# Second output block with six products by seven, second down block with sixteen; weight sums of three pairs by adding transfers

## The chip, the cores and the metric

The kernel runs on one core of one Trainium2 chip. The metric is the device time of one execution in microseconds, the median of several runs. A profiled execution gives the trace: its span goes from the first to the last instruction, and its own time is a little longer than the span.

## The reference

One layer of a hybrid block for 256 tokens of width 2048, all in fp32:

```python
h = rms_norm(x, g_mix);  proj = h @ w_in          # 2048 x (queries, keys, values, gates)
o_fox, o_sb, o_mem = three attentions over slices of proj
merged = g0 * (o_fox @ w_br_fox) + g1 * (o_sb @ w_br_sb) + g2 * (o_mem @ w_br_mem)
x = x + merged @ w_out                            # 2048 x 2048
h2 = rms_norm(x, g_ffn)
u = causal_depthwise_conv(h2 @ w_up, conv_w, conv_b)   # 2048 x 11264
u_gate, u_val = split(u)
return x + (silu(u_gate) * u_val) @ w_down        # 5632 x 2048
```

## The kernel before

All weights stream from memory in pieces of 128 rows by 1024 columns (0.5 MB in fp32). TensorE multiplies fp32 as two parts: ScalarE (ACT) makes the high part of a piece by a cast (`hi`), VectorE (DVE) the low part by a subtraction (`lo`), and each product of a 128x128 block of activations with a half piece of 512 columns is `three` matmuls: high by high, low activation by high weight, high activation by low weight. There are four buffers each for `hi` and `lo`, and six for the raw pieces.

The stages by the trace: projections, attentions and gates until about 659 us; the output stage `o` (merged @ w_out) in two blocks of 1024 columns, 659 to 700 and 700 to 742 us; the up stage `u` with its convolution, 742 to 1232 us, 176 pieces; the down stage `d` in two blocks, 1232 to 1344 and 1344 to 1455 us.

`blocked()` does a block of the stages `o` and `d`. It takes the weights' row tiles in pairs, 8 pairs in `o` and 22 in `d`, and a string, the plan, says for each pair in which way it is multiplied:

- `e`, `eight`: the 2x2 blocks of 128 tokens and 512 columns for two row tiles, 8 products, 24 matmuls; two pieces are loaded.
- `s`, `seven`: the same by seven products (after Strassen and Winograd), 21 matmuls of 128x512. It needs sums of weights T1 to T4 and sums of activations FS1 to FS4, and loads three and a half pieces: `raw0` (half a piece of weights and T3), `raw1`, `raw_t` (T1 and T2) and T4. Products go to four more PSUM banks Y, which `gather` adds to the output behind the last seven of a block.
- `f`, `form`: no product; it makes the sums of activations of the next pair (`pair_sums`: five steps on DVE with further splitting steps, and casts on ACT). In the output stage the sums of activations are made by `merged_sums` and `last_merged_sums`.

The weight sums do not depend on the activations. They are made beforehand, as background work, and kept in memory (`kept_...`): a pair's two pieces are loaded into SBUF (`pre_...`), DVE adds three times, and the four sums are stored. `halves` lists the pairs, output stage first; `first_sums`, `pair_sums_ahead` and `half_sums` work the list off, the last part of it during the up stage, one pair every 8 ticks (a tick there is one weight piece). All those transfers are issued by SyncE (SP) in one queue, the one that carries the weight pieces too.

In `o`'s second block the residual x of the first block is complete, and `hidden_T` transposes it (hT, 16 transposes on TensorE into four banks, read by ACT and DVE, L183 and L186, while ACT also squares x for the norm, L622); the four banks are then used for Y. Most instructions may be reordered by a scheduler; those in `in_order` stay where they are.

Of the kernel before, what the change touches and what calls it, by code (L numbers as in the profile page):

```python
# [10 lines left out]
F32 = mybir.dt.float32  # L11
F32R = mybir.dt.float32r
AF = mybir.ActivationFunctionType
ALU = mybir.AluOpType
AX = mybir.AxisListType

P = 128
# [16 lines left out]
PIECE = 1024  # L34
# [9 lines left out]
def hybrid_block(  # L44
# [25 lines left out]
    nc = tc.nc  # L70
# [31 lines left out]
    background = []  # L102
# [72 lines left out]
    def split_to(dst, src):  # L175

        nc.scalar.copy(dst[..., :S], src)
        nc.vector.tensor_tensor(dst[..., S:], src, dst[..., :S].bitcast(F32), ALU.subtract)
# [25 lines left out]
    def k_tiles(name):  # L204
# [19 lines left out]

    o_plans = ("eessssse", "eessssse")
    g_plans = (("", "esesesee", "esesesee"), ("esesesee", "esesesee", "esesesee"))
    d_plans = (
        "efefefef" + "sef" * 4 + "ssefsfssfssee",  # L230
        "efefef" + "sss" + "esss" * 3 + "ssee",
    )
    T1, T3, T4, T2 = range(4)
    FS2, FS4, FS3, FS1 = range(4)
    in_order = tc.keep_in_program_order
    dram = ctx.enter_context(tc.tile_pool(name="dram", bufs=1, space=bass.MemoryType.DRAM))
    by_k = lambda w: w[0].rearrange("(k p) n -> p k n", p=P)
    o_sevens = (0, 1, 2, 3, 6)
    pairs = lambda name, n: o_sevens if name == "o" else range(n)
    sums_of = {}  # L240
    ordered = [False]
    halves = deque(
# [1 line left out]
        for name, w, plans in (("o", w_out, o_plans), ("d", w_down, d_plans))  # L244
        for nb, plan in enumerate(plans)
        for pr in pairs(name, plan.count("s"))
        for h in range(2)
    )

# [35 lines left out]
    def pair_sums_ahead(staging, period, add, store, most=99, delay=0):  # L285

        due = deque()
        clock = 0
        for _ in range(delay):
            yield  # L290

        def step():
            while due and due[0][0] <= clock:
                _, kept, w = due.popleft()
                in_order(nc.sync.dma_start(kept, w))

        periods = cycle(period if isinstance(period, tuple) else (period,))
        while len(halves) > 1 and halves[0][-1] == 0 and most:
            most -= 1
            name, wv, nb, pr, _ = halves.popleft()  # L300
            halves.popleft()
            kept = kept_for(name, nb, pr)
            w = staging(f"pre_{name}{nb}_{pr}")
            in_order(
                nc.sync.dma_start(
                    w.rearrange("p (k c) -> p k c", k=2), wv[:, 2 * pr : 2 * pr + 2, nb * PIECE : (nb + 1) * PIECE]
                )
            )
            w = w.rearrange("p (i c) -> p i c", i=4)
            due.append((clock + store, kept, w))  # L310
            for t in range(next(periods)):
                if t == add:
                    sums_in(w)
                step()
                clock += 1
                yield
        while due:
            step()
            clock += 1
            yield  # L320

    def first_sums():

# [319 lines left out]
    def block(name, dt=F32):  # L643
        return bp.tile([P, 1024], dt, tag="blk", name=name)
# [409 lines left out]
    def last_merged_sums():  # L1054
        yield 2
        after = op.tile([P, KT, 2 * S], F32R, tag="ot", name="m_after")
        ms[6] = after[:, 0:2].rearrange("p k c -> p (k c)").rearrange("p (f l q) -> p f l q", f=4, l=2)
        pair_sums(mT[6], block("mw_6"), [(ms[6], slice(0, 4))])

    raw_g = lambda name: wp.tile([P, PIECE], F32, tag="raw", name=name)  # L1060

# [117 lines left out]
    for nb, plan in enumerate(o_plans):  # L1179
# [20 lines left out]
    background.append(  # L1200
        pair_sums_ahead(lambda name: ends_tile(name, F32).rearrange("p i c -> p (i c)"), 8, 1, 5, delay=DU)
    )

    def a_pair(p):
        if p < FA // 2:
            return aT[:, 2 * p : 2 * p + 2]
        if not ends:
            ends.append(ends_tile("a_ends", F32R).rearrange("p i (k c) -> p i k c", k=2))
        return ends[0][:, p - FA // 2]
# [22 lines left out]
    def taken(cr, y, f, s):  # L1232
        ct = s * FT + f
        u = pads[f % 2]
        ins = nc.vector.tensor_tensor(u[:, 2:], cr, rbc, ALU.mult)  # L1235
        if y is not None:
            in_order(ins)
        y = y_tile(f, s) if y is None else y
        tap = lambda j: taps[:, j, ct : ct + 1]
        nc.scalar.activation(y, u[:, 2:], AF.Identity, scale=tap(2), bias=tap(3))  # L1240
        nc.vector.scalar_tensor_tensor(y, u[:, 1 : S + 1], tap(1), y, ALU.mult, ALU.add)
        nc.vector.scalar_tensor_tensor(y, u[:, 0:S], tap(0), y, ALU.mult, ALU.add)
        if s == 0:
            nc.scalar.activation(y, y, AF.Silu)
            ys[f] = y
        else:
            g = ys.pop(f)
            nc.vector.tensor_tensor(g, g, y, ALU.mult)
            split_to(a_pair(f // 2)[:, f % 2], g)

    def conv(ps, f, s):
        taken(out_of(ps, cp.tile([P, S], F32, tag="cr", bufs=2, name=f"cr_{f}_{s}")), None, f, s)
# [66 lines left out]
    def s_of(p, f):  # L1319


        if f == FS1:
            return a_blocks[:, 2 * p, :, 1]
        if p < 9:
            return sf[:, 3 * p + f]
        if p == 9:
            return sf_more[0][:, f] if f < 2 else sf_rest[2]
        if p == 10:
            return sf[:, 27] if f == 0 else sf_rest[f - 1]
        return a_blocks[:, 2 * (p - N0 + N1) + f // 2, :, f % 2]  # L1330

    tmp_d = lambda name: place([P, PIECE], F32, "ts", name)

# [66 lines left out]
```

## Time and profile before

| | us |
|---|---|
| median of 3 runs | 1460.83 (1460.07 to 1462.5) |
| profiled execution, own time | 1460.56 |
| its span | 1458.8 |
| TensorE busy | 1452.1 |
| VectorE busy | 1221.8 |
| ScalarE busy | 851.9 |
| GpSimd busy | 21.4 |

The granted TensorE clock was 1.000. In the lines of the profile, `hi_o`, `lo_o`, `raw_o` are the pieces of the output stage, `_u` of the up stage, `_d` of the down stage, and `hi_t`, `lo_t`, `raw_t` the sums of weights. A group's line gives its count, busy time, mean duration of one, and the idle time of the engine ahead of it with what ended most of it. A line of the timeline gives start, duration and, in brackets, the engine's idle time before it and its releaser; the matmuls' ends are modelled and overlap the next starts.

### The profile page before, as it was taken

To read this page: it belongs to the slowest core of one execution; us is meant where nothing else is said; L and a number is where in the kernel's file an instruction comes from. 1 tells how busy PE (TensorE), PEld (TensorE's weight loads), DVE (VectorE), ACT (ScalarE), POOL (GpSimd) and SP (SyncE) were. 2 spreads that over 40 slices of the span, in tenths; PEclk is the share of its full clock that TensorE was granted. 3 is DMA by queue.
4 is the path that set the end of the run, shared out by engine and by line. 5 is a ranking of instruction groups with operands and counts; after the bars stand their busy time and mean duration, and the time that the engine had idled before them with its cause. 6 is when DMAs were issued, how large, how long until landed. Compare 5 with 4: busy or idle time off the path is not lost.

```text
span 1458.8 us, 20569 instructions
## 1 busy us (share of the span) xinstructions
PE 1452.1 (100%) x7295; PEld 1228.4 (84%) x7295; DVE 1221.8 (84%) x1804; ACT 851.9 (58%) x1210; POOL 21.4 (1%) x52
## 2 busy tenths in 40 slices
PE   9999999999999999999999999999999999999998
PEld 7888878888888888888888888888888888888887
DVE  5788778776898899998987888888888877999878
ACT  6755445464564555546766656556556565676665
POOL 0000010010000000000000000000000000000000
PEclk9999999999999999999999999999999999999999
DMA  8797899777668576788877888888888866789896
GB/s 290 228 352 247 320 323 333 266 250 217 212 206 268 176 226 201 271 266 261 304 213 231 290 275 299 282 270 299 286 278 298 272 197 201 253 283 341 293 334 220
DMA packets 166502, 387.64 MB, mean 266 GB/s; under 512 B 12554, under 2 KB 29854, under 8 KB 162174
## 3 DMA queue, kind: packets, MB, share of 16 engines
q1 hardware_dynamic: 164702, 383.29, 79.2%
q10 hardware_dynamic: 1328, 2.11, 0.4%
q8 instruction: 57, 0.93, 0.3%
q0 software_dynamic: 368, 0.93, 0.2%
q14 instruction: 47, 0.39, 0.1%
HBM read 347.47 MB, written 38.80 MB: 265 GB/s over the span
## 4 chain that ended last, share of the span: by engine, by line
PE 95%; issue 1%; DVE 1%; DMA 1%; SPq 0%; ACT 0%; POOL 0%; DVEq 0%; POOLq 0%; ACTq 0%
PE u L1289 22%; PE u L1290 11%; PE xg L362 4%; PE xg L361 4%; PE xg L360 4%; PE xd L360 4%; PE xd L362 3%; PE xd L361 3%; PE s L362 2%; PE f L360 2%; PE s L360 2%; PE f L362 2%; PE f L361 2%; PE b L362 2%; PE s L361 2%; PE b L361 2%
## 5 line engine op out<-in xcount | busy, mean ns | idle before, releaser
L1289 PE MATMUL u<-hT,hi_u 128*128 128x512 f32 x1232 | 428.5, 394 | 0.0
L1290 PE MATMUL u<-hT,lo_u 128*128 128x256 f32 x1232 | 341.5, 277 | 0.0
L1289 PEld LDWEIGHTS u<-hT,hi_u 128*128 128x128 f32 x1232 | 231.0, 188 | 53.4
L144 DVE TENSOR_TENSOR lo_u<-raw_u,hi_u 128x1024 fp32r<-128x1024 f32 x176 | 215.5, 1225 | 72.1 <-ACT hi_u L143 71.8
L143 ACT CAST hi_u<-raw_u 128x1024 fp32r<-128x1024 f32 x176 | 184.7, 1050 | 132.7 <-PE u L1289 107.0
L1290 PEld LDWEIGHTS u<-hT,lo_u 128*128 128x128 f32 x1232 | 231.5, 188 | 0.0
L355 DVE TENSOR_TENSOR lo_d<-raw_d,hi_d 128x1024 fp32r<-128x1024 f32 x88 | 106.8, 1223 | 16.7 <-ACT hi_d L354 14.3
L354 ACT CAST hi_d<-raw_d 128x1024 fp32r<-128x1024 f32 x88 | 91.8, 1053 | 39.9 <-PE xd L361 14.3
L354 ACT CAST hi_g<-raw_g 128x1024 fp32r<-128x1024 f32 (+1 forms) x80 | 77.0, 972 | 48.5 <-PE xg L361 19.2
L355 DVE TENSOR_TENSOR lo_g<-raw_g,hi_g 128x1024 fp32r<-128x1024 f32 (+1 forms) x80 | 88.7, 1121 | 4.1 <-ACT hi_g L354 4.1
L362 PE MATMUL xg<-lo_g,xT 128*128 128x512 f32 x175 | 68.1, 389 | 0.0
L360 PE MATMUL xg<-hi_g,xT 128*128 128x512 f32 x175 | 68.1, 389 | 0.0
L361 PE MATMUL xg<-hi_g,xT 128*128 128x512 f32 x175 | 68.1, 389 | 0.0
L143 ACT CAST hi_f<-raw_f 128x1024 fp32r<-128x1024 f32 (+1 forms) x40 | 38.5, 966 | 46.3 <-PE f L361 30.7
L144 DVE TENSOR_TENSOR lo_s<-raw_s,hi_s 128x1024 fp32r<-128x1024 f32 (+1 forms) x40 | 44.5, 1119 | 24.4 <-ACT hi_s L143 24.4
L1289 PE MATMUL u<-hT_rest,hi_u 128*128 128x512 f32 x176 | 62.0, 394 | 0.0
L143 ACT CAST hi_s<-raw_s 128x1024 fp32r<-128x1024 f32 (+1 forms) x40 | 38.4, 962 | 38.2 <-PE s L361 26.5
L143 ACT CAST hi_b<-raw_b 128x1024 fp32r<-128x1024 f32 x32 | 33.7, 1052 | 45.4 <-PE b L361 18.6
L1240 ACT ACTIVATE y<-u,taps 128x256 f32<-128x256 f32 x88 | 49.5, 595 | 17.0 <-DVE u L1235 16.8
L144 DVE TENSOR_TENSOR lo_f<-raw_f,hi_f 128x1024 fp32r<-128x1024 f32 (+1 forms) x40 | 44.4, 1117 | 16.9 <-ACT hi_f L143 16.9
L360 PE MATMUL xd<-hi_d,aT 128*128 128x512 f32 x148 | 57.6, 389 | 0.0
L362 PE MATMUL xd<-lo_d,aT 128*128 128x512 f32 x148 | 57.6, 389 | 0.0
(551 smaller groups left out, 3484.0 us busy)
## 6 DMA issues: line engine op xcount, KB each, us to landing
raw_u<-in_w_up_dram SPq DMA_DIRECT2D x176, 512.0 KB, 4.8
raw_g<-in_w_in_dram SPq DMA_DIRECT2D x96, 512.0 KB, 4.5
raw_d<-in_w_down_dram SPq DMA_DIRECT2D x63, 512.0 KB, 5.6
pre_d<-in_w_down_dram SPq DMA_DIRECT2D x17, 1024.0 KB, 7.2
kept_d<-pre_d SPq DMA_DIRECT2D x17, 1024.0 KB, 6.7
raw_f<-in_w_in_dram SPq DMA_DIRECT2D x32, 512.0 KB, 5.8
raw_s<-in_w_in_dram SPq DMA_DIRECT2D x32, 512.0 KB, 6.1
raw_t_d<-kept_d SPq DMA_DIRECT2D x25, 512.0 KB, 5.8
```

The lines of the kernel that those rows point to most:

```text
L143: pin(nc.scalar.copy(hi[:, :m], raw[:, :m]))
L144: pin(nc.vector.tensor_tensor(lo[:, :m], raw[:, :m], hi[:, :m].bitcast(F32), ALU.subtract))
L354: nc.scalar.copy(hi[:, :n], src)
L355: nc.vector.tensor_tensor(lo[:, :n], src, hi[:, :n].bitcast(F32), ALU.subtract)
L360: fix(nc.tensor.matmul(o, lhsT=ah, rhs=w[0], start=first, stop=False))
L361: fix(nc.tensor.matmul(o, lhsT=al, rhs=w[0], start=False, stop=False))
L362: fix(nc.tensor.matmul(o, lhsT=ah, rhs=w[1], start=False, stop=last))
L1240: nc.scalar.activation(y, u[:, 2:], AF.Identity, scale=tap(2), bias=tap(3))
L1289: nc.tensor.matmul(ps[i], lhsT=hi[:, j, c], rhs=hT(k + j), start=first, stop=False)
L1290: nc.tensor.matmul(ps[i][:, :S], lhsT=lo[:, j, c], rhs=hT(k + j)[:, :S], start=False, stop=last)
```

## The change

The plan of the output stage's second block gets a sixth seven (pair 5), the plan of the second down block two more sevens (16 for 14) in another arrangement with five forms for three; its last run of sevens has seven in a row (five before, and one form stands within it). `last_merged_sums` makes the sums of activations of pair 5 too. The weight sums of the second down block's pairs 13, 14 and 15 are made by a new background function, `sums_in_hbm`, on GpSimd's queue: for each pair a small copy that waits for an activation tile of the up stage, a copy of the pair's pieces from memory to memory, and four transfers that add to what lies there. The number of pairs that are summed through SBUF stays 35.

```diff
-    o_plans = ("eessssse", "eessssse")
+    o_plans = ("eessssse", "esssssse")
...
-        "efefef" + "sss" + "esss" * 3 + "ssee",
+        "efsss" * 3 + "efssfsssssee",
...
+    in_hbm = [("d", 1, pr) for pr in range(13, 16)]
...
-    o_sevens = (0, 1, 2, 3, 6)
-    pairs = lambda name, n: o_sevens if name == "o" else range(n)
+    o_sevens = {5: (0, 1, 2, 3, 6), 6: (0, 1, 2, 3, 6, 5)}
+    pairs = lambda name, n: o_sevens[n] if name == "o" else range(n)
...
+        if (name, nb, pr) not in in_hbm
...
+    def sums_in_hbm(period):
+        mark = cst.tile([P, 1], F32, tag="rows", name="mark")
+        for name, nb, pr in in_hbm:
+            while not a_done:
+                yield
+            in_order(nc.gpsimd.tensor_copy(mark, a_done[-1][:, :1].bitcast(F32)))
+            kept = kept_for(name, nb, pr)
+            b = by_k(w_down)[:, 2 * pr : 2 * pr + 2, nb * PIECE : (nb + 1) * PIECE]
+            b = b.rearrange("p k (n c) -> p k n c", n=2)
+            in_order(nc.gpsimd.dma_start(kept.rearrange("p (k n) c -> p k n c", k=2), b))
+            for dst, src in ((0, b[:, 0, 1]), (1, b[:, 1, 1]), (3, kept[:, 0]), (2, kept[:, 3])):
+                in_order(nc.gpsimd.dma_start(kept[:, dst], src, accum_op=ALU.add))
+            for _ in range(period):
+                yield
...
-        ms[6] = after[:, 0:2].rearrange("p k c -> p (k c)").rearrange("p (f l q) -> p f l q", f=4, l=2)
-        pair_sums(mT[6], block("mw_6"), [(ms[6], slice(0, 4))])
+        for i, p in enumerate((6, 5)):
+            ms[p] = after[:, 2 * i : 2 * i + 2].rearrange("p k c -> p (k c)")
+            ms[p] = ms[p].rearrange("p (f l q) -> p f l q", f=4, l=2)
+            pair_sums(mT[p], block(f"mw_{p}"), [(ms[p], slice(0, 4))])
+            yield 3
...
+    a_done = []
+    background.append(sums_in_hbm(24))
...
-            split_to(a_pair(f // 2)[:, f % 2], g)
+            a_done.append(a_pair(f // 2)[:, f % 2])
+            split_to(a_done[-1], g)
...
-        return a_blocks[:, 2 * (p - N0 + N1) + f // 2, :, f % 2]
+        i = 3 * (p - N0) + f
+        return a_blocks[:, 2 * N1 + i // 2, :, i % 2]
```

Three places show how instructions move. Lines of the changed kernel have other numbers (L371 for L354, L377 to L379 for L360 to L362, L639 for L622). The first place is ACT in the second output block, before: the casts of the second eight's pieces 10 and 11 and of the first seven's pieces 0 and 1 stand ahead of the reading of the transposes.

```order
L354 CAST hi_o_10_6429<-raw_o_10_6427 128x1024
L354 CAST hi_o_11_6447<-raw_o_11_6445 128x1024
L354 CAST hi_o_0_6476<-raw_o_0_6467 128x1024
L354 CAST hi_o_1_6486<-raw_o_1_6470 128x1024
L183 ACTIVATE hT<-hT_6383,gmix_c 128x256 x2
L183 ACTIVATE hT<-hT_6392,gmix_c 128x256 x2
L622 ACTIVATE junk_f_0_6401,ssf<-xres_again 128x512
L622 ACTIVATE junk_f_0_6403,ssf<-xres_again 128x512
L183 ACTIVATE hT<-hT_6405,gmix_c 128x256 x2
L183 ACTIVATE hT<-hT_6414,gmix_c 128x256 x2
L622 ACTIVATE junk_f_1_6423,ssf<-xres_again 128x512
L622 ACTIVATE junk_f_1_6425,ssf<-xres_again 128x512
```

The same place now, on ACT:

```order
L371 CAST hi_o_0_6447<-raw_o_0_6438 128x1024
L371 CAST hi_o_1_6457<-raw_o_1_6441 128x1024
L371 CAST hi_t_o_0_6467<-raw_t_o_0_6443 128x1024
L371 CAST hi_t_o_0_6477<-raw_t_o_0_6445 128x512
L183 ACTIVATE hT<-hT_6390,gmix_c 128x256 x2
L183 ACTIVATE hT<-hT_6399,gmix_c 128x256 x2
L639 ACTIVATE junk_f_0_6408,ssf<-xres_again 128x512
L639 ACTIVATE junk_f_0_6410,ssf<-xres_again 128x512
L183 ACTIVATE hT<-hT_6412,gmix_c 128x256 x2
L183 ACTIVATE hT<-hT_6421,gmix_c 128x256 x2
L639 ACTIVATE junk_f_1_6430,ssf<-xres_again 128x512
L371 CAST hi_o_2_6493<-raw_o_2_6484 128x1024
```

The four casts ahead of that work are now those of the first seven alone, and the second seven's first cast (piece 2) stands behind it (one more square stands between them, as before). The second place is PE, at the start of that second seven. Before:

```order
L360 MATMUL yo_0_6463<-hi_o_2_6522,mT_1_4411 128x512
L361 MATMUL yo_0_6463<-hi_o_2_6522,mT_1_4411 128x512
L362 MATMUL yo_0_6463<-lo_o_2_6523,mT_1_4411 128x512
L360 MATMUL yo_3_6466<-hi_o_2_6522,ms_5728 128x512
L361 MATMUL yo_3_6466<-hi_o_2_6522,ms_5728 128x512
L362 MATMUL yo_3_6466<-lo_o_2_6523,ms_5728 128x512
L360 MATMUL xo_0_0_6343<-hi_o_3_6532,mT_1_4411 128x512
```

And now:

```order
L377 MATMUL yo_0_6434<-hi_o_2_6493,mT_1_4411 128x512
L378 MATMUL yo_0_6434<-hi_o_2_6493,mT_1_4411 128x512
L377 MATMUL yo_3_6437<-hi_o_2_6493,ms_5728 128x512
L378 MATMUL yo_3_6437<-hi_o_2_6493,ms_5728 128x512
L377 MATMUL xo_0_0_6350<-hi_o_3_6503,mT_1_4411 128x512
L379 MATMUL yo_0_6434<-lo_o_2_6494,mT_1_4411 128x512
L379 MATMUL yo_3_6437<-lo_o_2_6494,ms_5728 128x512
```

The first matmul with a low part of weights (`lo_o_2`) moved from the third place to the sixth. The third place is SP's queue at the end of the second down block, where `raw_d` and `raw_t_d` are the pieces and sums loaded, and 40 to 43 the pieces of the two eights that end the block. Before:

```order
L447 DMA raw_d_26_13679<-in_w_down_dram 128x512
L448 DMA raw_d_26_13679<-kept_d_13_11046 128x512
L416 DMA raw_d_27_13682<-in_w_down_dram 128x1024
L451 DMA raw_t_d_13_13684<-kept_d_13_11046 128x2x512
L453 DMA raw_t_d_13_13686<-kept_d_13_11046 128x512
L416 DMA raw_d_40_13725<-in_w_down_dram 128x1024
L416 DMA raw_d_41_13743<-in_w_down_dram 128x1024
```

And now:

```order
L464 DMA raw_d_28_13718<-in_w_down_dram 128x512
L465 DMA raw_d_28_13718<-kept_d_14_8028 128x512
L433 DMA raw_d_29_13721<-in_w_down_dram 128x1024
L468 DMA raw_t_d_14_13723<-kept_d_14_8028 128x2x512
L470 DMA raw_t_d_14_13725<-kept_d_14_8028 128x512
L464 DMA raw_d_30_13764<-in_w_down_dram 128x512
L465 DMA raw_d_30_13764<-kept_d_15_8720 128x512
L433 DMA raw_d_31_13767<-in_w_down_dram 128x1024
L468 DMA raw_t_d_15_13769<-kept_d_15_8720 128x2x512
L470 DMA raw_t_d_15_13771<-kept_d_15_8720 128x512
L433 DMA raw_d_40_13810<-in_w_down_dram 128x1024
L433 DMA raw_d_41_13828<-in_w_down_dram 128x1024
```

Behind the seven of pair 13 the loads of two more sevens, pairs 14 and 15, come ahead of the two eights.

## The prediction

> **What bounds the kernel now.** I began with the page: busy shares, then the chain that ended last.
>
> ```profile
> PE 1452.1 (100%) x7295; PEld 1228.4 (84%) x7295; DVE 1221.8 (84%) x1804; ACT 851.9 (58%) x1210; POOL 21.4 (1%) x52
> PE 95%; issue 1%; DVE 1%; DMA 1%; SPq 0%; ACT 0%; POOL 0%; DVEq 0%; POOLq 0%; ACTq 0%
> ```
>
> TensorE (PE) is busy all the time, and 95% of the last chain is its own. So time changes only by matmuls that go, or by waits of PE that come. The second view is the windows by stage: the two column blocks of the output stage, the up stage, the down blocks, then two pieces of the second down block.
>
> ```profile
> core 0: us, PE busy (x) PEld busy (x) DVE busy (x) ACT busy (x) POOL busy (x), PEclk, DMA share, GB/s
> 658.90:699.70 40.80, 40.80 (x185) 33.81 (x184) 34.55 (x41) 26.67 (x30) 0.00 (x0) 1.00 0.85 283
> 699.96:742.20 42.24, 42.13 (x195) 34.92 (x194) 38.98 (x48) 30.46 (x44) 0.00 (x0) 1.00 0.84 278
> 742.20:1232.30 490.10, 490.10 (x2834) 429.00 (x2833) 408.91 (x668) 292.44 (x452) 1.29 (x2) 1.00 0.81 264
> 1232.30:1344.40 112.10, 112.10 (x496) 92.78 (x495) 107.79 (x168) 75.78 (x102) 0.00 (x0) 1.00 0.85 287
> 1344.40:1454.80 110.40, 110.40 (x493) 91.53 (x491) 92.17 (x108) 68.26 (x82) 0.00 (x0) 1.00 0.84 288
> 1412.00:1440.00 28.00, 28.00 (x125) 23.18 (x124) 22.11 (x20) 19.11 (x22) 0.00 (x0) 1.00 1.00 348
> 1408.00:1440.00 32.00, 32.00 (x143) 26.48 (x142) 25.76 (x24) 22.33 (x25) 0.00 (x0) 1.00 0.97 332
> 1424.00:1432.00 8.00, 8.00 (x37) 6.61 (x36) 7.14 (x8) 6.26 (x7) 0.00 (x0) 1.00 0.95 311
> ```
>
> PE lacks 0.11 us in the second output block and nothing in the down blocks, at full granted clock (1.00). The last three rows lie in the long run of sevens that ends the second down block: there the DMA engines are 95 to 100% busy. So the two rivals of PE are the DMA engines there, and, in the output stage, whatever stands in the way of ACT and DVE, which prepare each weight piece.
>
> Third, the timeline of PE gives the price of a matmul. Busy times (0.39) overlap; the starts tell:
>
> ```profile
> 1419.67 0.39 PE L362 MATMUL xd<-lo_d,aT 128*128 128x512 f32 x1
> ...
> 1421.03 0.39 PE L362 MATMUL yd<-lo_d,sf_rows 128*128 128x512 f32 x1
> ```
>
> Six steps from start to start make 1.36 us: 0.227 us for each matmul of 128x512. A seven (21 matmuls) takes PE 4.76 us, an eight (24) 5.44 us.
>
> **The change part by part.** Each eight turned into a seven frees three matmuls: 3 x 0.227 = 0.68 us. One in the output stage, two in the second down block: 0.68 + 1.36 = 2.04 us, 0.14% of the time. That is the most that the change can gain; what follows can only be taken from it.
>
> *Second output block.* Before, the transposes hT are followed by an eight, and its 5.44 us cover a block of ACT's work:
>
> ```profile
> 705.40 2.23 PE L197 MATMUL hT<-ident,xres_again 128*128 128x128 f32 x16
> 707.39 0.47 PE L360 MATMUL xo<-hi_o,mT 128*128 128x512 f32 x1
> 706.32 1.56 ACT L183 ACTIVATE hT<-hT,gmix_c 128x256 fp32r<-128x256 f32 x4
> 711.55 0.24 ACT L622 ACTIVATION_READ_ACCUMULATOR junk_f<-xres_again 128x1 f32 x1
> 711.64 1.08 ACT L354 CAST hi_t_o<-raw_t_o 128x1024 fp32r<-128x1024 f32 x1
> ```
>
> ACT reads the transposes from 706.32 and is free for the next weight piece at 711.64. PE multiplies four pieces cast earlier. After the change these four belong to one seven, 0.68 us shorter, and the seven behind it needs its first cast at 707.39 + 4.76 = 712.15, while that cast ends at 711.64 + 1.05 = 712.69: 0.54 us late. The low part, which DVE makes in 1.22 us after the cast, is there at 713.9. If PE asked for it in the third matmul, it would be due at 712.15 + 2 x 0.227 = 712.60, and PE would lose 1.3 us. The order of the changed kernel puts five matmuls with high parts ahead of the first with the low one: due at 712.15 + 5 x 0.227 = 713.28, 0.6 us late. That is what I take.
>
> The sums of activations of pair 5 add to DVE what those of pair 6 cost in the first output block:
>
> ```profile
> L378 DVE TENSOR_TENSOR m_after<-mw,m_after 128x512 fp32r<-128x512 f32 x1 | 0.7, 685 | 0.0
> L369 DVE TENSOR_TENSOR mw<-mT 128x512 f32<-128x512 f32 x1 | 0.7, 684 | 0.0
> L372 DVE TENSOR_TENSOR mw<-mw 128x256 f32<-128x256 f32 x1 | 0.4, 416 | 0.0
> L373 DVE SCALAR_TENSOR_TENSOR mw<-mw 128x128 f32<-128x128 f32 x1 | 0.3, 284 | 0.0
> L374 DVE TENSOR_TENSOR mw<-mw 128x128 f32<-128x128 f32 x1 | 0.3, 284 | 0.0
> ```
>
> Together 2.35 us, against 40.80 - 34.55 = 6.25 us in which DVE is idle there. Stepping DVE's rows through in the new order, all but 0.4 us falls into idle time; the rest delays the additions to xres that the transposes wait for. That moves transposes and casts alike, so it costs at most its 0.4 us. For this block: 0.6 us lost; bounds 0, if ACT comes to its block earlier by what PE saves, and 1.3 + 0.4 = 1.7.
>
> *Second down block: DVE and ACT.* Two more forms of sums and two sevens in place of eights. A form is the rows above (2.35 us); a seven needs 3.5 pieces of lo where an eight needs 2:
>
> ```profile
> L355 DVE TENSOR_TENSOR lo_d<-raw_d,hi_d 128x1024 fp32r<-128x1024 f32 x43 | 52.1, 1221 | 2.8 <-ACT hi_d L354 2.4
> ```
>
> So 1.5 x 1.22 = 1.8 us more each. DVE goes from 92.17 to about 92.2 + 2 x 2.4 + 2 x 1.8 = 100.6 us of 109, 92%. The first down block runs at 107.79 of 112.10, 96%, with eleven forms, and PE misses nothing there. Cost nothing; if this cover is gone, up to two forms, 4.7 us. ACT has more room (68.26 of 110.40).
>
> *Second down block: DMA.* A seven loads 3.5 pieces of 0.524 MB = 1.835 MB, an eight 1.05 MB. At the 332 GB/s of the long run a seven takes 5.53 us to load and 4.76 to multiply: it falls 0.77 us behind; an eight catches up over 2 us. Before, the last run has five sevens; now seven. Where the fifth stands:
>
> ```profile
> 1433.51 1.57 ACT L354 CAST hi_t_d<-raw_t_d 128x1024 fp32r<-128x1024 f32 x2 [0.30 <-PE yd L361]
> 1437.03 1.05 ACT L354 CAST hi_d<-raw_d 128x1024 fp32r<-128x1024 f32 x1 [0.42 <-DMA raw_d<-in_w_down_dram]
> 1438.96 1.57 ACT L354 CAST hi_t_d<-raw_t_d 128x1024 fp32r<-128x1024 f32 x2 [0.88 <-PE xd L361]
> 1440.05 1.83 DVE L355 TENSOR_TENSOR lo_t_d<-raw_t_d,hi_t_d 128x1024 fp32r<-128x1024 f32 x2 [0.71 <-ACT hi_t_d L354]
> 1442.15 0.39 PE L362 MATMUL yd<-lo_t_d,aT 128*128 128x512 f32 x1
> ```
>
> The casts of hi_t_d should be 4.76 us apart: 1433.51 + 4.76 = 1438.27, and the last comes at 1438.96, 0.69 us late, after a wait for a load at 1437.03. (Its own wait is put down to PE; I read it as its load, since the cast before found one late.) The low part is ready at 1440.05 + 1.22 = 1441.27, and PE takes it at 1442.15: 0.88 us are left. Two more sevens at 0.77 make 1.54; less 0.88, PE waits 0.66 us: I take 0.7. Bounds: 348 GB/s gives 5.27 us, 2 x 0.51 - 0.88 = 0.1 us; 311 GB/s gives 5.90, 2 x 1.14 - 0.88 = 1.4 us. The Trainium skill, "DMA: Bandwidth & Descriptors", section Specifications, gives a limit of about 358 GB/s between memory and one core; a seven would load in 5.13 us, and 2 x 0.37 = 0.74 would stay inside the 0.88, with no wait at all. The 348, 332 and 311 GB/s of this run lie below that limit, so here the sum goes by the rows.
>
> *Up stage.* Three groups of weight sums are no longer loaded, added and stored through SBUF, but three others take their place there, so SP and DVE keep their work. Pool, idle here (1.29 us of 490.10), gets three bursts, before the 20th, 44th and 68th weight piece or so (795, 862 and 929 us): a copy of 1.05 MB within memory and four adding transfers of 0.26 MB. Nothing queues behind Pool's own wait. What it can hurt is raw_u.
>
> ```profile
> L143 ACT CAST hi_u<-raw_u 128x1024 fp32r<-128x1024 f32 x173 | 181.6, 1050 | 131.0 <-PE u L1289 107.0 <-DMA raw_u<-in_w_up_dram 8.5 <-issue 7.1
> raw_u<-in_w_up_dram SPq DMA_DIRECT2D x176, 512.0 KB, 4.8
> kept_d<-pre_d SPq DMA_DIRECT2D x17, 1024.0 KB, 6.7
> ACT hi_u L143 <- DMA raw_u<-in_w_up_dram: 7.5, 2, 5.6
> ```
>
> ACT mostly waits for PE to hand back a buffer (107.0 us against 8.5 for loads): with four buffers, three pieces of 2.78 us (490.10 / 176) lie ahead when one comes free, and 8.34 less a cast of 1.05 and a low part of 1.22 leaves some 6 us. Once, near 773 us (last row: waits from 770 to 815 us), a cast waited 5.6 us for a load, and PE did not stop. DMA full rate here is 264 / 0.81 = 326 GB/s. A burst is 1.05 MB copied and 1.05 MB added; at that rate 6.4 us, or 9.6 us if an addition's reading of its destination counts too; within some 20 us the idle 19% take 3.8, which leaves raw_u 2.6 to 5.8 us late against 6 us. I take 0; bounds 0 and 1 us a burst.
>
> *Sum.* -2.04 + 0.6 + 0.7 + 0 = -0.74 us. The profiled execution took 1460.56 us (span 1458.8): 1459.8. It lies 0.27 under the median of the runs, 1460.83, so the median should be 1460.1. About 0.2% (2.9 us) is what a measurement of this kernel tells from no change: the forecast is "no difference".
>
> **The rivals.**
>
> 1. *Every cover holds.* The transposes' block of ACT is met by matmuls that come in another order, and the loads reach 348 GB/s or more. Against it: the casts late by 0.69. Time: 1460.83 - 2.04 = 1458.8.
>
> 2. *Slower: adding transfers hold up raw_u.* An adding transfer reads its destination, adds and writes; no row shows its price. If its 1.05 MB per burst go at a fourth of the full rate, a burst is 3.2 + 4 x 3.2 = 16 us of the DMA engines; the idle 19% of some 30 us take 5.7, so raw_u falls 10.3 us behind, and PE waits 10.3 - 6 = 4.3 us, three times: 12.9. Half that rate (3.2 + 6.4 = 9.6, less 3.8) stays inside the 6 us. It decides above some three times the price: 3.2 + 9.6 - 4.5 = 8.3, a wait of 2.3 a burst, 6.9 in all, so 1460.1 + 6.9 = 1467.0. For it: the loads share the 16 engines (0.81), and the 5.6 us row shows how one late load eats the reserve. Against it: PE stood that without a stop, and bursts lie 67 us apart. The Trainium skill, same page, section Queues, rings and completion order, says that each DMA engine serves the queues with work in turn, packet by packet; by that rule Pool's burst would take up to half of every engine while it lasts. The trace, with one queue in use there, cannot show it.
>
> 3. *Slower, but little: both stalls at their upper bounds,* 1.7 + 1.4, and 1 us in the up stage: -2.04 + 4.1 = +2.1, 1462.9.
>
> **How the numbers follow.** Forecast and its surroundings (1459.2 to 1461.7): 0.47, for each of its terms is read from a row. Rival 1: 0.19. Rival 3 (1461.7 to 1463.7): 0.12. Rival 2: 0.22. The low end is rival 1 less the 0.4 us by which runs differ, 1458.4; the high end is rival 3 plus one burst's 1 us and more, 1464.3, which leaves out most of rival 2. Faster by over 0.2% (under 1457.9) is beyond the 2.04 us: 0.03 for scatter. Slower by over 0.2% (above 1463.75): 0.24. Within: 0.73.
>
> **What would show it.** The windows of after: in the second output block a PE gap of about 0.6 us in the second seven, released by DVE's low part or ACT's cast. In the last run of sevens, ACT's waits for raw_d and raw_t_d in the sixth and seventh, and PE idle up to 1.4 us there. In the up stage no PE gap at 795 to 815 us, though waits of hi_u for raw_u. PE gaps of over 1 us there, thrice, are rival 2; no gap anywhere, rival 1. A time under 1458 or over 1464 makes the forecast wrong.

## The result and the profile after

| | before | after |
|---|---|---|
| median, us (9 runs each) | 1460.83 (1459.92 to 1462.50) | 1471.62 (1465.41 to 1472.76) |
| profiled execution, us | 1460.56 | 1469.28 |
| its span, us | 1458.8 | 1467.6 |

The ratio is 1.0061 (95% interval 1.0051 to 1.0071): slower by 0.6%, by the medians 10.8 us. Forecast were 1460.1 and "no difference", within 1458.4 to 1464.3. The nine runs of the changed kernel lie in groups: three at 1465.4 to 1466.2 us, five at 1471.6 to 1472.8, and the profiled one between them. Only that one was traced, so how the parts below add up in the others is not known. Ratios leave out one run, of the first candidate below, whose granted clock was 0.753 (1804 us).

The page of the changed kernel, engine totals, queues and chain:

```profile
PE 1459.5 (99%) x7286; PEld 1229.4 (84%) x7286; DVE 1230.8 (84%) x1831; ACT 858.5 (58%) x1225; POOL 35.7 (2%) x70
q0 software_dynamic: 2912, 7.22, 2.2%
PE 88%; DMA 5%; DVE 3%; issue 2%; ACT 1%; SPq 0%; POOL 0%; ACTq 0%; DVEq 0%; POOLq 0%
```

DMA has entered the chain, and PE is busy longer although it has fewer matmuls. The windows by stage say where (second output block, up stage, first and second down block, cut where each stage's first matmul starts):

```profile
core 0: us, PE busy (x) PEld busy (x) DVE busy (x) ACT busy (x) POOL busy (x), PEclk, DMA share, GB/s
700.55:743.00 42.45, 42.31 (x191) 33.74 (x190) 39.87 (x51) 31.61 (x45) 0.00 (x0) 1.00 0.86 292
743.00:1242.39 499.39, 497.88 (x2833) 431.89 (x2832) 408.60 (x667) 292.16 (x451) 15.29 (x20) 1.00 0.84 272
1242.39:1354.69 112.30, 112.30 (x497) 92.94 (x496) 107.91 (x168) 75.89 (x102) 0.00 (x0) 1.00 0.86 289
1354.69:1463.00 108.31, 108.31 (x483) 89.81 (x482) 98.31 (x127) 73.44 (x94) 0.00 (x0) 1.00 0.87 305
```

The up stage takes 499.39 us for 490.10: 9.3 us more, with 2833 matmuls in the trace for 2834. The first down block is unchanged. From the start of the second down block to the end of the span it is 1467.6 - 1354.69 = 112.9 us, before 1458.8 - 1344.40 = 114.4: 1.5 us gained. The second output block lost 0.2. What the change was said to touch least carries the whole loss.

The 9.3 us have two parts. First, PE stops. The second burst of transfers on GpSimd's queue began at 850.8 us. SP's queue in that time, after (first four rows) and before (last four); a row is a run of issues, with start, duration and count:

```profile
853.53 0.34 SPq L297 DMA_DIRECT2D kept_d<-pre_d  x1
854.67 1.50 SPq L142 DMA_DIRECT2D raw_u<-in_w_up_dram  x2
863.00 0.37 SPq L307 DMA_DIRECT2D pre_d<-in_w_down_dram  x1
863.46 16.35 SPq L142 DMA_DIRECT2D raw_u<-in_w_up_dram  x6
...
850.50 0.34 SPq L295 DMA_DIRECT2D kept_d<-pre_d  x1
851.90 3.14 SPq L142 DMA_DIRECT2D raw_u<-in_w_up_dram  x2
856.51 0.37 SPq L305 DMA_DIRECT2D pre_d<-in_w_down_dram  x1
857.45 14.46 SPq L142 DMA_DIRECT2D raw_u<-in_w_up_dram  x6
```

The staged sums have one buffer in SBUF. The load of the next pair (`pre_d`) waits in SP's queue until the store of the last (`kept_d`) has landed, and the weight pieces (`raw_u`) stand behind it. Before, the store took until 856.51, six microseconds after its issue; beside a burst, it takes until 863.00, 9.5 us, and SP issues no piece from 856.2 to 863.46. The three stores beside bursts took 8.9 to 10.2 us until the next load was issued, the others 6.2 to 7.5, as before (4.5 to 7.6). The waits of the up stage, of after and then of before (total, times, longest), show it over the whole stage:

```profile
SPq L307 <- DMA kept_d<-pre_d: 52.0, 16, 6.8
ACT hi_u L143 <- DMA raw_u<-in_w_up_dram: 56.4, 33, 4.8
...
SPq L305 <- DMA kept_d<-pre_d: 27.7, 15, 2.6
```

The casts waited 8.5 us in three places for their loads before; now 56.4 in 33. Once the reserve is gone (chain, cast, low part, and the two matmuls around the gap; the bracket is the idle time and its releaser):

```profile
863.46 10.55 DMA raw_u<-in_w_up_dram
874.12 2.20 ACT L143 CAST hi_u<-raw_u 128x1024 fp32r<-128x1024 f32 x2 [3.96 <-DMA raw_u<-in_w_up_dram]
875.20 1.23 DVE L144 TENSOR_TENSOR lo_u<-raw_u,hi_u 128x1024 fp32r<-128x1024 f32 x1 [3.79 <-ACT hi_u L143]
875.22 0.50 PE L1312 MATMUL u<-hT_rest,hi_u 128*128 128x512 f32 x1
876.48 0.39 PE L1313 MATMUL u<-hT_rest,lo_u 128*128 128x256 f32 x1 [0.76 <-DVE lo_u L144]
```

The piece issued at 863.46 is there 10.55 us later, and PE stands 0.76 us between a high and a low part. The same happens at 968 us, after the third burst. Both together lengthen four pieces by 2.7 us.

The second part, 6.6 us, has no gap at all. Here are 120 us of the up stage without a stop, before and after:

```profile
1100.00:1220.00 120.00, 120.00 (x694) 104.99 (x693) 100.65 (x170) 72.52 (x114) 0.00 (x0) 1.00 0.76 244
...
1100.00:1220.00 120.00, 120.00 (x681) 104.07 (x680) 96.92 (x159) 68.41 (x105) 0.00 (x0) 1.00 0.77 249
```

681 matmuls for 694 in the same time, at the same granted clock (1.00), with the bursts long past. Both steps are longer: from a high part's matmul to the low part's 236 ns for 232, and back 117 for 115. By the starts of the pieces, each takes PE 2.773 us up to the stop at 876 us, as in the kernel before, and 2.826 from there to the end of the stage: 0.053 x some 124 pieces = 6.6 us.

### The profile page after: what moved, and what is told of

Read it like the earlier page. It is cut to its first block, busy times and chain, and to the rows that moved or that the text cites. A ratio compares the mean times of both kernels' runs of the same rounds, so it can differ in the third digit from the quotient of the medians.

```text
span 1467.6 us, 20659 instructions
## 1 busy us (share of the span) xinstructions
PE 1459.5 (99%) x7286; PEld 1229.4 (84%) x7286; DVE 1230.8 (84%) x1831; ACT 858.5 (58%) x1225; POOL 35.7 (2%) x70
## 4 chain that ended last, share of the span: by engine, by line
PE 88%; DMA 5%; DVE 3%; issue 2%; ACT 1%; SPq 0%; POOL 0%; ACTq 0%; DVEq 0%; POOLq 0%
PE u L1312 19%; PE u L1313 10%; PE xd L377 3%; PE xd L379 3%; PE xd L378 3%; PE xg L379 3%; PE xg L378 3%; PE xg L377 3%; DMA raw_u<-in_w_up_dram 3%; PE s L379 2%; PE f L379 2%; PE s L377 2%; PE f L377 2%; PE f L378 2%; PE s L378 2%; PE b L378 2%
## 5 line engine op out<-in xcount | busy, mean ns | idle before, releaser
L1312 PE MATMUL u<-hT,hi_u 128*128 128x512 f32 x1232 | 434.5, 397 | 0.0
L1313 PE MATMUL u<-hT,lo_u 128*128 128x256 f32 x1232 | 345.0, 280 | 0.0
L371 ACT CAST hi_d<-raw_d 128x1024 fp32r<-128x1024 f32 x88 | 91.7, 1053 | 35.9 <-PE xd L378 11.9
L371 ACT CAST hi_g<-raw_g 128x1024 fp32r<-128x1024 f32 (+1 forms) x80 | 77.1, 972 | 49.1 <-PE xg L378 19.2
L377 PE MATMUL xg<-hi_g,xT 128*128 128x512 f32 x175 | 68.1, 389 | 0.0
L379 PE MATMUL xg<-lo_g,xT 128*128 128x512 f32 x175 | 68.1, 389 | 0.0
L371 ACT CAST hi_t_d<-raw_t_d 128x1024 fp32r<-128x1024 f32 (+1 forms) x54 | 43.5, 835 | 19.3 <-PE xd L378 12.1
L371 ACT CAST hi_t_g<-t_g 128x1024 fp32r<-128x1024 f32 x30 | 31.5, 1051 | 39.0 <-PE xg L378 34.0
```

The costliest lines, as they stand in the source:

```text
L371: nc.scalar.copy(hi[:, :n], src)
L377: fix(nc.tensor.matmul(o, lhsT=ah, rhs=w[0], start=first, stop=False))
L379: fix(nc.tensor.matmul(o, lhsT=ah, rhs=w[1], start=False, stop=last))
L1312: nc.tensor.matmul(ps[i], lhsT=hi[:, j, c], rhs=hT(k + j), start=first, stop=False)
L1313: nc.tensor.matmul(ps[i][:, :S], lhsT=lo[:, j, c], rhs=hT(k + j)[:, :S], start=False, stop=last)
```

## The experiments

Ratios are against the kernel before, measured beside each run. "Pace" is what a weight piece takes PE in the up stage in the profiled run, 2.77 or 2.83 us.

**Bursts alone, and the plans with other sums.** The first adds only GpSimd's bursts to the kernel before, for pairs 14 to 16, whose sums nobody reads; the second leaves them out of the changed kernel and makes the three pairs' sums through SBUF, faster:

```diff
+    in_hbm = [("d", 1, pr) for pr in range(14, 17)]
...
+    background.append(sums_in_hbm(24))
```
```diff
-    in_hbm = [("d", 1, pr) for pr in range(13, 16)]
+    in_hbm = []
...
-        pair_sums_ahead(lambda name: ends_tile(name, F32).rearrange("p i c -> p (i c)"), 8, 1, 5, delay=DU)
+        pair_sums_ahead(lambda name: ends_tile(name, F32).rearrange("p i c -> p (i c)"), (7, 7, 7, 7, 6), 1, 5, delay=DU)
```

> The kernel before with GpSimd's three bursts added (for pairs 14 to 16 of the second down block, whose sums nobody reads); plans and staged sums as before. Theory A (the bursts make raw_u late, PE stops in the up stage, and after the first stop each weight piece takes 2.826 us instead of 2.773 until the stage ends): 6 to 12 us slower than before, 1467 to 1473, with at least one PE gap of about 0.8 us in the up stage and pieces of 2.83 us behind it. Rival B (the new plans or the other layout of the program slow the up stage): as before, 1460.8, pieces of 2.77 us throughout.

1470.24 us, 1.0065 (1.0042 to 1.0088): the bursts alone cost about what the change costs. Three stops at 874 to 879 us, at a low, a high and a low part; in the profiled run (1466.59, the fastest of four) the pace behind them was 2.77, against theory A, but for 3.4 us in which the granted clock was 0.50.

> The changed kernel without GpSimd's transfers: the weight sums of all pairs go through SBUF on SP's queue (one pair in 6.8 ticks instead of 8). Theory A: no stop in the up stage, pieces of 2.77 us; the matmuls' gain of 2.04 us less 0.9 lost in the second output block: 1459.7. Rival B: 1468 or more, pieces of 2.83 us.

1480.48 us, 1.0133 (1.0118 to 1.0148): worse still, which neither expected. Eight stops at low parts, 13.3 us in all; the pace went to 2.83 and back. So the second route is no way out, and the run says nothing on the plans.

```profile
PEld u L1313 <- DVE lo_u L144: 13.3, 8, 4.1
```

**Does any stop set the slow pace?** Idle work ahead of one piece's cast on ACT, no transfers added, at piece 48 and at piece 120:

```diff
+                late = (f0, s, k) == (12, 0, 0)
...
+                if late:
+                    for _ in range(22):
+                        in_order(nc.scalar.copy(idle, idle))
                 hi, lo = piece(upv[:, k : k + 2, c0 : c0 + 512], 2, 512, f"u{f0}_{s}_{k}")
```

> The kernel before with 22 idle copies on ACT (some 10.5 us) ahead of the cast of up-stage piece 48; no transfer is added. Theory A (any stop starts the slow rhythm): one stop of some 2 us, then 127 pieces x 0.053 = 6.7 us: 1469.5. Rival C (the slow rhythm comes from transfers in memory, not from the stop): the stop alone, 1463, pieces of 2.77 us behind it.

> The same 22 idle copies ahead of piece 120. Theory A: a stop of some 2 us, then 55 x 0.053 = 2.9 us: 1465.7, 3.8 us less than with piece 48. Rival C: 1463, the same as with piece 48.

1469.31 (1.0066, 1.0041 to 1.0091) and 1471.24 us (1.0070, 1.0050 to 1.0089). PE stopped longer than planned, and behind each stop the granted clock was 0.50 for 6.8 us; the pieces around the stop take about 8 and 9 us more in all. The earlier stop cost no more than the later one, and once the clock was back the pace was 2.77 behind both. The stop at piece 48, a window right behind it (the clock stands before the last two numbers) and one far behind it:

```profile
883.29 1.22 PE L1296 MATMUL u<-hT,hi_u 128*128 128x512 f32 x2 [5.05 <-ACT hi_u L143]
884.00:887.00 3.00, 2.96 (x10) 2.16 (x9) 3.00 (x7) 3.00 (x5) 0.00 (x0) 0.50 0.45 106
1100.00:1220.00 120.00, 120.00 (x694) 104.94 (x693) 98.62 (x164) 69.92 (x107) 0.00 (x0) 1.00 0.79 251
```

Theory A falls: a stop ahead of a high part does not change the pace. The changed kernel's own stops, some 1 us each, brought no such stretch of the clock. Next, DVE's idle work makes the low part alone late, with 11 steps at piece 48 and 13 at piece 120:

```diff
+                    for _ in range(11):
+                        in_order(nc.vector.scalar_tensor_tensor(idle, idle, 1.0, idle, ALU.mult, ALU.mult))
```

> The kernel before with 11 idle steps on DVE (some 6 us and what stands with them) ahead of the low part of up-stage piece 48; no transfer is added, and the high part is in time. Theory A2 (a stop at a low part alone, between the 512 and the 256 wide matmul, puts PE into the slow rhythm; a stop at the high part does not): a stop of 1 to 3 us, then pieces of 2.83 us, 127 x 0.053 = 6.7: 1468.5 to 1470.5. Rival C: the stop alone, 1462 to 1464, pieces of 2.77 us behind it.

> The same with 13 idle steps ahead of the low part of piece 120. Theory A2: a stop of 1 to 3 us, then 55 x 0.053 = 2.9: 1465 to 1467. Rival C: 1462 to 1464.

1469.85 (1.0068, 1.0047 to 1.0089) and 1468.21 us (1.0046, 1.0030 to 1.0062). The stops were longer than expected (1.38 and 4.95 us; 4.1), and at the two long ones the granted clock was 0.50 for 6.8 and 3.4 us, so the times alone don't decide. The pace does: behind the stop at piece 48 it is 2.83 to the end of the stage; with the stop at piece 120 it is 2.77 up to there and 2.83 behind. Rows: the second stop at piece 48, matmuls in the window of piece 120's run ahead of its stop, and behind it:

```profile
890.49 1.22 PE L1297 MATMUL u<-hT,lo_u 128*128 128x256 f32 x4 [4.95 <-DVE lo_u L144]
990.00:1050.00 60.00, 60.00 (x348) 52.49 (x347) 51.68 (x84) 35.43 (x56) 0.00 (x0) 1.00 0.86 287
1100.00:1220.00 120.00, 120.00 (x681) 104.03 (x680) 97.74 (x162) 68.90 (x105) 0.00 (x0) 1.00 0.77 249
```

A stop at a low part sets the slow pace with no transfer added: it is PE's own, and not memory's. One thing more changed with the late step, though: in that piece the program has four matmuls with high parts and then four with low ones (the x4 of the first row), where other pieces alternate (with the late cast it is two and two). That order alone did not do it where it stands without a stop: in the candidate with the shorter period (below) two neighbouring pieces at 840 to 846 us have such groups, the first two and two, the second four and four, with the quick pace ahead of them and behind. And in the changed kernel all pieces alternate. It is no strict law either: of the eight such stops in the run with faster staging, one was followed by the quick pace; in the run with bursts alone the last of the three stops was at a low part and left it quick; and three waits of 0.2 to 0.3 us at low parts (two in the first candidate and one in the first run with spread transfers, both below) left it quick too. In the run with faster staging and the candidate with the shorter period the pace came back to quick five times, three of them with no stop, and each time at a piece whose matmuls don't alternate.

**What the plans are worth.** Both plans without transfers, then the down plan alone; three pairs read other pairs' sums, so that nothing of them is made:

```diff
-    background.append(sums_in_hbm(24))
...
+    for _, nb, pr in in_hbm:
+        sums_of["d", nb, pr] = sums_of["d", nb, pr - 3]
```

> The changed kernel with both plans and no transfers for pairs 13 to 15: the sums of these three pairs are left out (the sums of pairs 10 to 12 are read in their place). If GpSimd's transfers are the whole loss: no stop in the up stage, pieces of 2.77 us, 42.4 us for the second output block, 108.3 for the second down block: before less 2.0 plus 0.9, about 1459.7. If the plans slow the up stage by themselves: over 1463.

> The kernel before with the new plan of the second down block alone, without transfers for pairs 13 to 15 (their sums are left out, those of pairs 10 to 12 are read). If the down block gains its two sevens whole: 1.36 us under before, 1459.1. If the load of the long run of sevens costs what was forecast (0.7): 1459.8. Against the run of both plans without sums (1460.1) it tells what the output stage's seven costs or brings.

1460.11 us (1.0002, 0.9990 to 1.0015) and 1458.96 us (0.9990, 0.9981 to 0.9998). Pace 2.77 in both. So the whole loss is the price of making three pairs' sums; the second down block brings its 1.36 us in full, and the output stage's seven brings nothing that shows: by the medians the run with it is 1.2 us longer, and the intervals overlap. Two of its twelve runs took 1463.5 and 1470.3 us, with none of these transfers; they were not traced, and what delayed them is open.

**Is it the adding, or the burst?** Bursts as in the first run, with plain copies for the four additions:

```diff
-                in_order(nc.gpsimd.dma_start(kept[:, dst], src, accum_op=ALU.add))
+                in_order(nc.gpsimd.dma_start(kept[:, dst], src))
```

> The kernel before with three bursts for pairs that nobody reads, as in the run with bursts alone, but the four adding transfers of each replaced by plain copies of the same 256 KB. In the changed kernel the additions took about 7 us of all 16 engines per burst, the copy 3. If the price of adding is what stops PE: no stop, 1461. If a burst of any kind does it: 1465 to 1472, as with additions.

1460.98 us, 1.0011 (0.9997 to 1.0024): no stop in the profiled run. GpSimd's queue between 745 and 1000 us, additions (the first run) and copies (packets, MB, share of the 16 engines):

```profile
q0 software_dynamic: 2624, 6.42, 11.5%
q0 software_dynamic: 1856, 6.42, 7.5%
```

255 us x 11.5% / 3 = 9.8 us of all engines per burst with additions, 6.4 with copies. Half of a burst is a copy in both, 3.2 us; so 1.05 MB take 6.6 us added and 3.2 copied: twice the price. SP waited as long for stores in both:

```profile
SPq L306 <- DMA kept_d<-pre_d: 54.0, 16, 6.4
SPq L306 <- DMA kept_d<-pre_d: 54.2, 16, 6.6
```

So in the profiled run the waits of SP alone do not stop PE, though the low part of one piece was ready only 0.4 us ahead of its matmul; with the dearer additions on top they do. The reserve lies between the two, and it is thin: two of the ten runs with copies took 1468.2 and 1469.7 us; they were not traced.

**Spreading them, and moving them.** Each pair's work in eight transfers of 256 KB, each released by a word of DVE's, five pieces apart; with both plans, and with the down plan alone. Then the same in the gates stage:

```diff
+            for i, (dst, src, how) in enumerate(steps):
+                go = cst.tile([P, 1], F32, tag="go", bufs=2, name=f"go_{pr}_{i}")
+                in_order(nc.vector.memset(go, 0.0))
+                in_order(nc.gpsimd.tensor_copy(mark, go))
+                in_order(nc.gpsimd.dma_start(kept[:, dst], src, **how))
```

> The changed kernel with each pair's transfers as eight of 256 KB (four copies, four additions), each started five weight pieces (14 us) after the last by a word that DVE writes. If the loss is the crowding of a burst: no stop in the up stage, 1459.7, faster than before by about 0.1%. If the adding transfers cost too much in whatever order: stops again, 1464 or more.

> The spread transfers with the new plan of the down stage alone; the output stage as before. If spreading works: before less 1.36 us, 1459.5, and 0.2 us better or the same as with both plans, since the second output block gained nothing from its seven (42.45 us for 42.24). If not: 1464 or more.

> The changed kernel with the eight 256 KB transfers of each pair in the gates stage (360 to 600 us), one with every third weight piece of the gates; nothing of them is left in the up stage. In the kernel before the DMA engines are 61 to 67% busy there, against 81% in the up stage, and three pairs need some 30 us of all 16 engines. If the up stage's crowding is the loss: no stop in the up stage, 1460.1 as without the sums, or up to 0.5 us less. If the gates' pieces are late in their turn: stops of PE there, 1462 or more.

1464.75 (1.0033, 1.0020 to 1.0047), 1465.70 (1.0035, 1.0023 to 1.0047) and 1467.89 us (1.0044, 1.0030 to 1.0058). Spreading takes half the loss away, no more. With both plans the twelve runs reach from 1461.0 to 1471.3 us; the traced one is the shortest, with one wait of 0.3 us and the quick pace throughout. One short wait is left in the down plan's run, and yet the pace is slow:

```profile
PEld u L1317 <- DVE lo_u L144: 0.3, 1, 0.3
1100.00:1220.00 120.00, 120.00 (x682) 103.99 (x681) 97.28 (x165) 70.45 (x109) 3.55 (x4) 1.00 0.76 240
```

There the slow pieces began at 990 us, ahead of that wait and without a gap between matmuls. What the trace shows there is a late weight load (PEld). A low part's load otherwise starts together with the matmul ahead of it (first two rows); at 990 us the low part was ready only at 990.14, and its load started 0.11 us behind that matmul:

```profile
989.74 0.39 PE L1316 MATMUL u<-hT_rest,hi_u 128*128 128x512 f32 x1
989.74 0.19 PEld L1317 LDWEIGHTS u<-hT_rest,lo_u 128*128 128x128 f32 x1
988.92 1.22 DVE L144 TENSOR_TENSOR lo_u<-raw_u,hi_u 128x1024 fp32r<-128x1024 f32 x1
990.08 0.39 PE L1316 MATMUL u<-hT,hi_u 128*128 128x512 f32 x1
990.19 0.19 PEld L1317 LDWEIGHTS u<-hT,lo_u 128*128 128x128 f32 x1
990.31 0.28 PE L1317 MATMUL u<-hT,lo_u 128*128 128x256 f32 x1
```

The matmul came 0.23 us behind its forerunner, as ever, and the pace was slow from that piece on. In the run with faster staging a slow stretch also began at such a load, 0.06 us late (1126 us). So a low part that is nearly late can be enough; that it must be is not shown. In the gates stage PE stands for low parts and for the releasing words instead (PE busy 235.87 of 240 us, before 240.00); idle transfer engines were no proof of room there.

**Turning the order.** The first low part of a piece ahead of its first high part, in 7 of 8 pieces: with a late low part, with spread transfers, in the changed kernel, and as a control in the kernel before:

```diff
-                        nc.tensor.matmul(ps[i], lhsT=hi[:, j, c], rhs=hT(k + j), start=first, stop=False)
-                        nc.tensor.matmul(
+                        high = lambda: nc.tensor.matmul(ps[i], lhsT=hi[:, j, c], rhs=hT(k + j), start=first, stop=False)
+                        low = lambda: nc.tensor.matmul(
                             ps[i][:, :S], lhsT=lo[:, j, c], rhs=hT(k + j)[:, :S], start=False, stop=last
                         )
+                        for product_of in (low, high) if k and i + j == 0 else (high, low):
+                            product_of()
```

> The kernel before with one pair of matmuls turned in each weight piece of the up stage (but the first piece of each bank group): the first low part (256 wide) before the first high part, so that a piece whose low part is late stops PE ahead of the piece and not between a 512 and a 256 wide matmul; with 11 idle steps on DVE ahead of the low part of piece 50. If the place of the stop decides the rhythm: a stop of 1 to 5 us, then pieces of the same length as ahead of it. If any stop at a low part does it: pieces longer by 0.05 us behind it.

> The new plan of the down stage with spread transfers, the output stage as before, and the turned pair in each piece. If the slow rhythm was the loss of the run with spread transfers (1465.7): 1459.0 of the run without sums, and up to 1 us of stops: 1459 to 1460.5, faster than before. If the turned pair costs time itself, the control run shows it.

> The changed kernel with the turned pair in each piece. If the rhythm is the larger part of the loss: the stops alone remain, 1460.1 of the run without sums and 2 to 4 us: 1462 to 1464, against 1471.6. If the rhythm isn't mended so: 1468 or more.

> Control: the kernel before with the turned pair and nothing else. No stop, pieces of 2.77 us: 1460.5. If the turned order has a rhythm of its own, the pieces show it.

1483.07 (1.0151, 1.0137 to 1.0165), 1467.15 (1.0043, 1.0030 to 1.0055), 1469.18 (1.0059, 1.0047 to 1.0072), and the control 1467.52 us (1.0042, 1.0028 to 1.0056). The control missed its expectation: with this order a turned piece takes 2.82 us, with no stop (and the eighth, which keeps the old order, 2.80), and that alone costs 6.5 us. Its 120 us, for 694 matmuls in the kernel before:

```profile
1100.00:1220.00 120.00, 120.00 (x684) 104.42 (x683) 97.04 (x162) 69.58 (x106) 0.00 (x0) 1.00 0.77 247
```

So the remedy fails, and the first of the four tells nothing on the place of a stop (PE stood there for two pieces, once for the high part). But the control gives a ground on which the pace is slow for all: on it, the whole change costs 1469.18 - 1467.52 = 1.7 us and the spread version of the down plan -0.4. So far as this ground stands for the slow pace of the old order, most of the change's 10.8 us is the pace, as in the profiled run (6.6 of 9.3 us).

**Candidates.** The down plan with all sums through SBUF, the output stage as before; started after 8 pieces instead of 22 (`DU`) at the old period, or after 17 with a shorter period:

```diff
-        pair_sums_ahead(lambda name: ends_tile(name, F32).rearrange("p i c -> p (i c)"), 8, 1, 5, delay=DU)
+        pair_sums_ahead(lambda name: ends_tile(name, F32).rearrange("p i c -> p (i c)"), 8, 1, 5, delay=8)
```
```diff
+        pair_sums_ahead(lambda name: ends_tile(name, F32).rearrange("p i c -> p (i c)"), (8, 7), 1, 5, delay=17)
```

> A candidate: the new plan of the second down block with all weight sums made through SBUF (19 pairs in the up stage for 17), nothing on GpSimd, the output stage as before; to make room the background work starts after 8 weight pieces instead of 22, with a period of 8 as before. If a period of 8 is what keeps SP's queue free: no stop, 1459.0 as without the sums, faster than before. If the two more pairs make raw_u late at the start of the stage: stops there and the slow pace behind them, 1468 or more.

> The same, but the background work starts after 17 pieces and takes 8 and 7 pieces in turn. If a shorter period by itself blocks SP's queue (a pair's load waits for the last pair's store): stops as with a period of 6.8 (1480), though fewer: 1465 to 1475. If not: 1459.0.

1459.51 us (1.0003, 0.9990 to 1.0015) and 1479.11 us (1.0133, 1.0119 to 1.0148). Two pairs more in both, and 20 us between them: with the shorter period and the later start PE stops seven times, 11.5 us in all. The first candidate beats the changed kernel; it isn't told apart from the kernel before. Its median is 0.9 us lower, but in single runs it came to 1462 to 1467 us, as a slow pace in part of the stage would give.

## Why the prediction was wrong

- **The step that failed** is the up stage, "I take 0; bounds 0 and 1 us a burst". It cost 9.3 us in the profiled run. Rival 2 had the mechanism (raw_u held up by the adding transfers, PE stops at the bursts' ends), with a chance of 0.22, but its terms were mis-sized. *Price:* an addition is twice a copy's, and 9.8 us a burst (bursts alone) is near the 9.6 that were said to "stay inside the 6 us". *Reserve:* the 6 us were the usual case; in the kernel before, a piece's low part is ready 5.9 us ahead of PE's first matmul with it by the median over the stage, but 2.0 us at 776 us. And a burst also slows the store on which SP's queue stands, so raw_u was late by up to 6.8 us of SP's waiting besides. The prediction said "Nothing queues behind Pool's own wait" and left out what queues behind SP's: the row of the changed length was `kept_d<-pre_d`, which it quoted only as a price. *Result:* two stops of 0.76 us, far less than the 4.3 a burst of rival 2, and then a slow pace, which was no term at all. (Rival 3 also counted the bound of 1 us once; for three bursts it is 3 us, which gives 1464.9, already above the range.)
- **The Trainium skill's rule** that each DMA engine serves the queues with work in turn ("DMA: Bandwidth & Descriptors", section Queues, rings and completion order) fits the stores that took 8.9 to 10.2 us instead of some 6 beside a burst; the share per packet was not measured.
- **Matmuls removed:** right. 0.227 us each; the second down block gained 1.5 us (1.36 forecast), also alone (1458.96 against 1460.48).
- **The long run of sevens:** 0.7 us of waiting were taken, bounds 0.1 and 1.4; there was none. Loads came late only to the extent of these waits between 1420 and 1455 us:

```profile
ACT hi_d L371 <- DMA raw_d<-kept_d: 0.6, 1, 0.6
ACT hi_d L371 <- DMA raw_d<-in_w_down_dram: 0.3, 1, 0.3
ACT hi_t_d L371 <- DMA raw_t_d<-kept_d: 0.2, 1, 0.2
```

  The 0.69 us of lateness before stood at the fifth seven and was taken as growing with every further one. (Whether that cast waited for its load, as was read, or for PE, as its row says, is not settled.) It did not grow over seven. The term that was mis-sized is the rate: through the new run the engines moved 347 GB/s, where 332 was taken from a window of the old one. By the prediction's own sum 347 leaves 0.2 us of waiting:

```profile
1408.00:1452.00 44.00, 44.00 (x196) 36.41 (x195) 38.08 (x41) 32.88 (x40) 0.00 (x0) 1.00 0.97 347
```

- **DVE's two forms more:** right, at nothing; DVE is busy 98.31 of 108.31 us there (100.6 of 109 forecast).
- **Second output block:** the sum was near (0.68 gained, 0.9 lost where 0.6 was taken), the place wrong. ACT's block did end late, and the second seven's first cast is ready just as PE wants it; the longest gap behind the transposes comes at the fifth seven, whose low part is late because its cast waited (rows: that first cast and PE's first matmul with it, the fifth seven's cast, the matmuls around the gap):

```profile
711.95 2.03 ACT L371 CAST hi_o<-raw_o 128x1024 fp32r<-128x1024 f32 x2
713.17 0.41 PE L377 MATMUL yo<-hi_o,mT 128*128 128x512 f32 x1
...
725.98 2.24 ACT L371 CAST hi_o<-raw_o 128x1024 fp32r<-128x1024 f32 x2 [1.43 <-DVE lo_t_o L372]
727.88 0.39 PE L378 MATMUL yo<-hi_o,mT 128*128 128x512 f32 x1
728.34 0.50 PE L379 MATMUL yo<-lo_o,mT 128*128 128x512 f32 x1
```

  From 727.88 to 728.34 are 0.46 us where 0.23 is the rule. The rest is some 0.1 us each right behind the transposes and at several places in the first two sevens.

## What to carry to other kernels

When background transfers are added, look at what stands in an in-order queue behind a wait for a landing: a transfer that merely takes longer holds every load behind it, and the reserve to compare with is its lowest value, not its median. Price an adding transfer higher than a copy; here it cost twice as much. And in a stage that PE fills without a gap, a single stop can cost more behind it than in it: compare how many matmuls equal windows hold ahead of and behind a stop before calling the stop the loss.

## What the runs showed of the hardware

- PE has two lasting paces for the same matmuls (512 and 256 wide in turn) at the same granted clock: 694 or 681 in 120 us. Stops at a low part alone mostly led into the slow one; the two stops ahead of a high part did not. It can tip with no gap between matmuls, where a low part's weight load came 0.06 and 0.11 us late, and tip back, five times where matmuls of a piece stood in another order; a turned order had nearly the slow pace (684) throughout. What in PE holds the pace is not settled.
- Behind or beside stops of PE of 4 us and more in the up stage the granted clock was 0.50 for 3.4 or 6.8 us (runs with a late cast or a late low part), so such a stop costs more than its own length.
- A transfer that adds to memory took 6.6 us of all 16 engines per 1.05 MB, a copy within memory 3.2.
- Staged pairs 8 and 7 pieces apart in turn, instead of 8, cost 20 us between the two candidates (the later start differs too): with one buffer, the store's landing holds the queue.
